# A two-layer diffusion block on one core: output weights a block ahead into four result banks, one operand sum by feature tiles, and slots of their own for the mixer's sums

## The chip, the cores and the metric

The kernel runs on 1 core of one Trainium2 chip. The metric is device time in microseconds (us) of one execution; the median of three runs is quoted. Engines are called as the profile calls them: PE is TensorE (its matmuls), PEld its weight loads, DVE is VectorE, ACT is ScalarE, POOL is GpSimd and SP is SyncE, whose queue (SPq) issues all of the loads and stores that matter here.

## The reference, cut to what matters

Two layers run over 1024 latent tokens and 256 context tokens of width 1024. The mixers of a layer (attention, mLSTM, neighbourhood) stay as they are; the change lies behind them.

```python
def trunk_layer(x, ctx, ...):
    ...
    x = x + gt1 * mix_out([ya, yb, yc, yd], g_group, w_out)      # output projection, 1024x1024
    h2 = rms_norm(x, g2) * (1 + sc2) + sh2
    x = x + gt2 * conv_ffn(h2, w_up, conv_w, conv_b, w_down)     # up 1024 -> 5632, conv, gate, down 2816 -> 1024
    if need_ctx:                                                 # layer 0 alone
        ctx = ctx + gt1c * mix_out([yac, ybc, ycc, ydc], g_group, w_out)
        h2c = rms_norm(ctx, g2) * (1 + sc2c) + sh2c
        ctx = ctx + gt2c * conv_ffn(h2c, w_up, conv_w, conv_b, w_down)
    return x, ctx

def conv_ffn(h, w_up, conv_w, conv_b, w_down):
    u = dwconv_centred(h @ w_up, conv_w, conv_b)                 # width 3, along the tokens
    gate, val = jnp.split(u, 2, axis=-1)
    return (jax.nn.silu(gate) * val) @ w_down
```

## The kernel before

Every number is kept as a high and a low part, and each product is three matmuls (`mm3`: L112 high by high, L113 the weights' high part by the data's low one, L114 the weights' low part by the data's high one). A high part is a cast on ACT, a low part a subtraction on DVE or POOL.

A layer has four stages. The first makes the projections and the mixers. **Phase 3** is the output projection with the second norm. **up** is the mixer's first product, and **down** its second.

Phase 3 (`out_span`) goes by spans of tokens: first 512 latent tokens, then 256, then the last 256 (`rest`), and in layer 0 the 256 context tokens (`cs`). For a span it loads the mixers' outputs (`yi`), transposes them on PE (`yt`), splits them (`yh`, `yl`), and then makes eight result tiles `o`, one for each feature tile f. A result tile needs two blocks of weights: a load `raw` (L100), a cast `wohi` on ACT (L103), a subtraction `wolo` on POOL or DVE (L104), in three buffers. DVE adds each result to the residual `xT` (L1476), SP stores that (L1478).

Behind a span come the norm's sums: squares `nsq` on ACT (L239), their sums over features on PE (`ssq` L243, `ss` L249), then `nms` on DVE, `nrs` on POOL (L253), `ndg` on DVE (L264), and `rsbc` on PE (L265), which spreads the factor. `scaled` then multiplies on DVE (L1489) and adds on ACT (L1490).

The up product is a Strassen form: per block j of 128 hidden features (22 of them) seven products b, of operands 11, 21, T1, T2, 22, T3, T4. T1, T2, T3 and T4 are differences of token and feature quarters. `combine` makes the parts of them that the last 512 tokens give, in two halves of 256 tokens; half 1 (`late`) belongs to `rest`. In layer 0 the context's result tiles run between the steps of half 1, in layer 1 nothing does. `kept` copies a product's bank to a tile `u` on ACT (L1588), which the later sums and the convolution read (L1602); `u` has six buffers in up's own pool.

down loads the gated values back (`graw`, L1665) with the weights (L1672) and the residual of all tokens (`xT<-sX`, eight loads at L1690), multiplies, and adds each result tile to `xT` (L1702). It works in groups of 2, 4, 4, 4, 4, 2 and 2 blocks. Up's last block and down's first tiles stand mixed in every queue. The eight result banks `b` are shared by both.

The order on each engine is static: a scheduler orders the program by priorities and its own estimates before it runs. Buffers are pools on a stack with a left and a right side; a tile that is laid over memory of a pool that is closed waits for the last users of those bytes. `xT` of down lies on the right side, where the operands 11 and 21 and up's late slots lay.

Of the kernel before, what the change touches and what calls it, by code (L numbers as in the profile page):

```python
# [7 lines left out]
F32 = mybir.dt.float32  # L8
# [7 lines left out]
P = 128  # L16
D = 1024
KD = 8
# [30 lines left out]
class Net:  # L49
# [1318 lines left out]
    def open_phase3(self, l):  # L1368
        self.spans = ([(0, 256, 1, 1024)] if self.need_ctx else []) + [(256, 768, 0, 0), (768, 1280, 0, 512)]
        self.p3 = [ExitStack() for _ in range(4)]  # L1370
        self.ring, self.late, self.made, self.B = {}, [], 0, {}
        self.operand(self.p3[2], "right", 11, 21)
        self.open_x()
        self.nrm = self.sb(self.p3[0], f"n2{l}", side="right")
        self.p3s = self.sb(self.p3[1], f"p3{l}", side="right")
        self.p3l = self.sb(self.p3[3], f"p3l{l}", side="right")
        self.p3p = self.ps(self.p3[1], f"p3m{l}", side="right")

    def operand(self, stack, side, *names):
        for b in names:  # L1380
# [3 lines left out]
    def phase3(self, l, modT):  # L1384
        spans = self.spans
        with ExitStack() as st:
            B, hc = self.B, None
# [10 lines left out]
            h = (t1 - t0) // 2  # L1398
            for _ in self.out_span(l, modT, (t0, t0 + h, v, c), (0,)):
                pass  # L1400
            rest = self.out_span(l, modT, (t0 + h, t1, v, c), (1,), (self.nc.gpsimd, self.nc.vector))
            next(rest)
            cs = self.out_span(l, modT, spans[0], None, (self.nc.gpsimd, self.nc.vector), hc) if hc else iter(())
# [11 lines left out]
            self.p3[1].close()  # L1415
            self.operand(st, None, "T4")
            few = self.need_ctx
            for x, n in (("raw", 4), ("s", 3), ("w", 3)) if few else (("raw", 4), ("s", 3), ("w", 6)):
                self.slots(st, x, n)
            with ExitStack() as mst:  # L1420
                self.slots(mst, "b", 6, "right", True)
                for half in (early, late):
                    for _ in half:
                        pass
                if hc:
                    self.norm2(l, modT, spans[0], lambda k: (hc[0][:, k], hc[1][:, k]))
                self.p3[0].close()
                self.xst.close()
                pst.close()
                self.slots(mst, "b", 2, None, True)  # L1430
                with ExitStack() as s2:
                    for x, n in (("raw", 2), ("w", 3)) if few else (("raw", 3), ("s", 1)):
                        self.slots(s2, x, n, "right", later=True)
                    self.up(l, B, hc, self.sb(s2, f"mu{l}", side="right"))
                self.p3[2].close()
                st.close()
                self.ring = {"b": self.ring["b"]}
                self.open_x()
                self.down(l, modT)

    def out_span(self, l, modT, span, homes, engs=None, home=None):
# [10 lines left out]
        for s0, long in zip(range(t0, t1, 256), homes or (1,)):  # L1452
            yh, yl = home or ((rp if long else self.p3l).tile([P, KD, 256], F32R, tag=x, name=x, bufs=1 if long else 2) for x in ("yh", "yl"))
            for i in range(s0 // P, s0 // P + 2):
                yi = self.p3l.tile([P, D], F32, tag="yi", name="yi", bufs=2)
                nc.sync.dma_start(yi, self.sY[i])
                cs = slice(i * P - s0, (i + 1) * P - s0)
                for g in range(2):
                    t = pm.tile([P, 4, P], F32, tag="yt", name="yt", bufs=1)
                    for j in range(4):  # L1460
                        nc.tensor.transpose(t[:, j], yi[:, (4 * g + j) * P:(4 * g + j + 1) * P], self.ident)
                    self.split(yh[:, 4 * g:4 * g + 4, cs], yl[:, 4 * g:4 * g + 4, cs], t)
            Y.append((yh, yl))
        yield
        for f in range(KD):
            W = []
            for x in range(2):
                hi, lo = self.weight(rp, a["w_out"][l, x * 512:(x + 1) * 512, f * P:(f + 1) * P]
                                     .rearrange("(k p) f -> p k f", p=P), engs[x], 3, "wo", 3)
                W += [(hi[:, k * P:(k + 1) * P], lo[:, k * P:(k + 1) * P]) for k in range(4)]  # L1470
            o = pm.tile([P, 512], F32, tag="o", name="o", bufs=2)
            for s, (yh, yl) in enumerate(Y):
                for k in range(KD):
                    self.mm3(o[:, s * 256:(s + 1) * 256], [(W[k], (yh[:, k], yl[:, k]))], k == 0, k == KD - 1)
# [1 line left out]
            nc.vector.scalar_tensor_tensor(out=xs, in0=o[:, 0:n], scalar=modT[:, 16 + f, v:v + 1], in1=xs,  # L1476
                                           op0=ALU.mult, op1=ALU.add)
            nc.sync.dma_start(self.sX[:, f, t0:t1], xs)  # L1478
            yield

    def scale2(self, modT, v):
# [35 lines left out]
    def combine(self, l, modT, B, half):  # L1517
# [7 lines left out]
        def sub(eng, out, a, b):  # L1525
            eng.tensor_tensor(out, a, b, ALU.subtract)

        def parts(b, x, eng):
            self.parted(x, *(y[:, :, c] for y in B[b]), eng)

        v = self.spans[-1][2]
        xs = self.xT[:, :, 768 + 256 * half:1024 + 256 * half]
        sc2 = self.scale2(modT, v)
# [2 lines left out]
        for k in range(4):  # L1536
            self.scaled(modT, xs, bc, sc2, v, k)
        yield
        sub(V, X[0, 0], X[0, 1], X[0, 0])
        yield  # L1540
        parts("T1", X[0, 0], V)
        yield
        for k in range(4, 8):
            self.scaled(modT, xs, bc, sc2, v, k)
# [15 lines left out]
    def up(self, l, B, hc, up):  # L1560
# [23 lines left out]
            self.mm3(o, [(W[k], (b[0][:, k], b[1][:, k])) for k in range(4)], first, skip_group_check=True)  # L1584

        def kept(o):
            s = up.tile([P, 512], F32, tag="u", name="u", bufs=6)
            nc.scalar.copy(out=s, in_=o)  # L1588
            return s

# [213 lines left out]
```

## Time and profile before

| what | value |
|---|---|
| median of 3 runs | 3404.1 us (3390.17 to 3408.64) |
| the profiled execution | 3407.24 us, span 3405.5 us |
| mean granted clock of PE | 0.978 |
| PE, DVE, ACT, POOL busy | 3257.6, 2215.4, 1503.2, 965.1 us |
| phase 3 of layer 0, of layer 1 (about) | 776 to 988 us, 2500 to 2696 us |
| up of layer 0, of layer 1 (about) | 988 to 1558 us, 2696 to 3152 us |

The span is what the profiler saw of the program; the execution's own time has 1.7 us around it. Busy time is the time in which an engine had an instruction under way. The granted clock is 1.0 at the upper of PE's two levels and 0.5 at the lower, so a mean between them says that PE ran a part of the stretch at the lower. All times of rows count from the span's start.

### The profile page before, as it was taken

What the parts mean: (1) busy time and instruction counts of PE and PEld (TensorE: products, weight loads), DVE (VectorE), ACT (ScalarE), POOL (GpSimd) and SP (SyncE); (2) the same over time, 40 slices, a digit from 0 to 9 for tenths busy, and PEclk for the clock granted to TensorE, in tenths of its full rate; (3) what the DMA queues carried; (4) which work ended last, traced back from release to release, by engine and by line L of the source; (5) the groups of instructions that cost most, each with busy time, mean ns of one, the idle gap of its engine ahead of it and who ended that gap; (6) DMA issues with size and microseconds to landing.
All of it is one profiled execution on the core that took longest, in us unless ns stands there. A gap on an engine that the chain in (4) does not pass through costs nothing. (4 is left out here: it accounts for less than half of the span.)

```text
span 3405.5 us, 55249 instructions
## 1 busy us (share of the span) xinstructions
PE 3257.6 (96%) x20699; PEld 2735.0 (80%) x20699; DVE 2215.4 (65%) x4141; ACT 1503.2 (44%) x3037; POOL 965.1 (28%) x1067
## 2 busy tenths in 40 slices
PE   7999999999979999999999899999999799999998
PEld 4798877878868888888887698878878678888886
DVE  4456654775578777777445656645774788888755
ACT  4345424566645444443111444424575544444321
POOL 1534424231552222210000624424313623332000
PEclk8999999999989999999999999999999899999999
DMA  7624445233532221216212534246144322223521
GB/s 288 198 74 138 147 131 159 69 106 120 161 101 70 75 67 61 78 52 238 91 62 99 152 100 135 72 130 155 55 135 128 111 78 90 75 86 117 186 82 59
DMA packets 412243, 385.87 MB, mean 113 GB/s; under 512 B 118088, under 2 KB 355784, under 8 KB 405832
## 3 DMA queue, kind: packets, MB, share of 16 engines
q1 hardware_dynamic: 411976, 382.34, 35.7%
q8 instruction: 163, 2.67, 0.3%
q14 instruction: 104, 0.85, 0.1%
HBM read 287.88 MB, written 94.37 MB: 112 GB/s over the span
## 5 line engine op out<-in xcount | busy, mean ns | idle before, releaser
L1702 DVE SCALAR_TENSOR_TENSOR xT<-b,modT,xT 128x512 f32<-128x512 f32 (+1 forms) x280 | 191.5, 695 | 202.8 <-PE b L114 202.2
L113 PE MATMUL b<-g,w 128*128 128x512 f32 (+1 forms) x880 | 321.9, 368 | 0.0
L114 PE MATMUL b<-g,w 128*128 128x512 f32 (+1 forms) x880 | 320.8, 368 | 0.0
L112 PE MATMUL b<-g,w 128*128 128x512 f32 (+1 forms) x880 | 320.1, 368 | 0.0
L112 PE MATMUL pj<-whi,hh 128*128 128x512 f32 (+2 forms) x800 | 286.1, 359 | 12.3 <-ACT v L535 6.2
L113 PE MATMUL pj<-wlo,hh 128*128 128x512 f32 (+2 forms) x800 | 281.0, 352 | 4.1 <-DVE wlo L104 4.1
L114 PE MATMUL pj<-whi,hl 128*128 128x512 f32 (+2 forms) x800 | 278.9, 350 | 0.0
L1573 POOL TENSOR_TENSOR s<-raw 128x512 f32<-128x512 f32 x88 | 117.8, 1338 | 485.1 <-DVE w L1580 397.3
L112 PEld LDWEIGHTS pj<-whi,hh 128*128 128x128 f32 x800 | 155.7, 195 | 45.4 <-ACT v L535 9.2
L113 PEld LDWEIGHTS b<-g,w 128*128 128x128 f32 x880 | 165.6, 189 | 27.5
L112 PEld LDWEIGHTS b<-g,w 128*128 128x128 f32 x880 | 165.5, 189 | 27.6
L114 PEld LDWEIGHTS b<-g,w 128*128 128x128 f32 x880 | 165.3, 188 | 27.6
L113 PEld LDWEIGHTS pj<-wlo,hh 128*128 128x128 f32 x800 | 156.1, 195 | 24.0 <-DVE wlo L104 5.0
L1602 DVE SCALAR_TENSOR_TENSOR cg<-u,vec,cg 128x512 f32<-128x512 f32 (+1 forms) x176 | 166.5, 989 | 10.0 <-ACT cg L1597 10.0
L87 ACT CAST w<-raw 128x512 fp32r<-128x512 f32 x88 | 53.6, 619 | 269.8 <-PE b L114 244.1
L1580 DVE TENSOR_TENSOR w<-raw,w 128x512 fp32r<-128x512 f32 x156 | 135.8, 885 | 54.7 <-ACT w L1579 54.7
L114 PEld LDWEIGHTS pj<-whi,hl 128*128 128x128 f32 x800 | 154.9, 194 | 20.3 <-issue 1.7
L1579 ACT CAST w<-s 128x512 fp32r<-128x512 f32 x176 | 107.0, 618 | 144.4 <-PE b L114 99.9
L104 POOL TENSOR_TENSOR wolo<-raw,wohi 128x512 fp32r<-128x512 f32 x88 | 119.2, 1357 | 151.4 <-ACT wohi L103 118.2
L114 PE MATMUL o<-yh,wolo 128*128 128x256 f32 x512 | 150.8, 296 | 8.3 <-POOL wolo L104 4.8
L112 PE MATMUL o<-yh,wohi 128*128 128x256 f32 x512 | 148.4, 291 | 8.8 <-ACT wohi L103 6.4
L113 PE MATMUL o<-yl,wohi 128*128 128x256 f32 x512 | 147.6, 289 | 0.0
(371 smaller groups left out, 9800.9 us busy)
## 6 DMA issues: line engine op xcount, KB each, us to landing
wmod<-in_w_mod_dram SPq DMA_DIRECT2D x48, 1024.0 KB
raw<-in_w_up_dram SPq DMA_DIRECT2D x176, 256.0 KB
raw<-in_w_out_dram SPq DMA_DIRECT2D x112, 256.0 KB
raw<-in_w_down_dram SPq DMA_DIRECT2D x88, 256.0 KB
raw<-in_w_in_dram SPq DMA_DIRECT2D x80, 256.0 KB
sG<-cv SPq DMA_DIRECT2D x22, 640.0 KB
graw<-sG SPq DMA_DIRECT2D x22, 640.0 KB
sG<-cv SPq DMA_DIRECT2D x22, 512.0 KB
```

What stands on the lines that cost most here:

```text
L87: nc.scalar.copy(out=hi, in_=src)
L104: eng.tensor_tensor(lo[:, 0:w], raw[:, 0:w], f32v(hi[:, 0:w]), ALU.subtract)
L112: nc.tensor.matmul(out, lh, rh, start=(first and i == 0), stop=False, **kw)
L113: nc.tensor.matmul(out, lh, rl, start=False, stop=False, **kw)
L114: nc.tensor.matmul(out, ll, rh, start=False, stop=(last and i == n - 1), **kw)
L1573: nc.gpsimd.tensor_tensor(s, x, y, op)
L1579: nc.scalar.copy(out=hi, in_=src)
L1580: nc.vector.tensor_tensor(out=lo, in0=src, in1=f32v(hi), op=ALU.subtract)
L1602: nc.vector.scalar_tensor_tensor(out=o[:, x0:x1], in0=u[:, x0 - d - c:x1 - d - c], scalar=self.cw[w][:, j:j + 1], in1=o[:, x0:x1], op0=ALU ...
L1702: nc.vector.scalar_tensor_tensor(out=xs, in0=o[:, 0:t1 - t0], scalar=modT[:, 40 + f, v:v + 1], in1=xs, op0=ALU.mult, op1=ALU.add)
```

## The change

It has four edits. The weights of result tile f+1 are made ahead of the matmuls of tile f, and have four buffers where they had three (the loads keep their three). The result tiles `o` have two banks, and from `rest` on two more in a pool `p3o`, by turns; the loads `yi` come as halves of 128x512, two buffers of that size, 36 loads where there were 18. For half 1 the difference T1 is made by feature tiles of 256 tokens, subtraction, cast and subtraction apiece, instead of one subtraction of 128x1024 and one split. The six buffers of `u` become slots: two on the left with the other slots, four on the right in the stack `s2`, below the late slots of `raw`, `w` and `s`; layer 0 has two `s` slots at first and one late where it had three at first.

```diff
+        self.p3o = [self.p3p]
...
             for _ in self.out_span(l, modT, (t0, t0 + h, v, c), (0,)):
                 pass
+            self.p3o += [self.ps(self.p3[1], f"p3o{l}", side="right")]
...
-            for x, n in (("raw", 4), ("s", 3), ("w", 3)) if few else (("raw", 4), ("s", 3), ("w", 6)):
+            for x, n in (("raw", 4), ("s", 2), ("w", 3), ("u", 2)) if few else (("raw", 4), ("s", 3), ("w", 6), ("u", 2)):
                 self.slots(st, x, n)
...
                 with ExitStack() as s2:
-                    for x, n in (("raw", 2), ("w", 3)) if few else (("raw", 3), ("s", 1)):
+                    self.slots(s2, "u", 4, "right")
+                    for x, n in (("raw", 2), ("w", 3), ("s", 1)) if few else (("raw", 3), ("s", 1)):
                         self.slots(s2, x, n, "right", later=True)
...
-                yi = self.p3l.tile([P, D], F32, tag="yi", name="yi", bufs=2)
-                nc.sync.dma_start(yi, self.sY[i])
                 cs = slice(i * P - s0, (i + 1) * P - s0)
                 for g in range(2):
+                    yi = self.p3l.tile([P, 512], F32, tag="yi", name="yi", bufs=2)
+                    nc.sync.dma_start(yi, self.sY[i, :, g * 512:(g + 1) * 512])
                     t = pm.tile([P, 4, P], F32, tag="yt", name="yt", bufs=1)
                     for j in range(4):
-                        nc.tensor.transpose(t[:, j], yi[:, (4 * g + j) * P:(4 * g + j + 1) * P], self.ident)
+                        nc.tensor.transpose(t[:, j], yi[:, j * P:(j + 1) * P], self.ident)
...
-        for f in range(KD):
+
+        def weights(f):
             W = []
             for x in range(2):
                 hi, lo = self.weight(rp, a["w_out"][l, x * 512:(x + 1) * 512, f * P:(f + 1) * P]
-                                     .rearrange("(k p) f -> p k f", p=P), engs[x], 3, "wo", 3)
+                                     .rearrange("(k p) f -> p k f", p=P), engs[x], 4, "wo", 3)
                 W += [(hi[:, k * P:(k + 1) * P], lo[:, k * P:(k + 1) * P]) for k in range(4)]
-            o = pm.tile([P, 512], F32, tag="o", name="o", bufs=2)
+            return W
+
+        W = weights(0)
+        for f in range(KD):
+            then = weights(f + 1) if f < KD - 1 else None
+            o = self.p3o[f % len(self.p3o)].tile([P, 512], F32, tag="o", name="o", bufs=2)
...
+            W = then
             yield
...
+        def fine(b, x, y):
+
+            for k in range(4):
+                sub(V, x[:, k], y[:, k], x[:, k])
+                self.parted(x[:, k], *(z[:, k, c] for z in B[b]), V)
+
...
-        sub(V, X[0, 0], X[0, 1], X[0, 0])
+        if half:
+            fine("T1", X[0, 0], X[0, 1])
+        else:
+            sub(V, X[0, 0], X[0, 1], X[0, 0])
         yield
-        parts("T1", X[0, 0], V)
+        if not half:
+            parts("T1", X[0, 0], V)
...
         def kept(o):
-            s = up.tile([P, 512], F32, tag="u", name="u", bufs=6)
+            s = self.slot("u", [P, 512])
             nc.scalar.copy(out=s, in_=o)
             return s
```

Since the scheduler orders anew, instructions move at three places that the diff doesn't show.

**PE at the end of the first span, layer 0.** The last result tile of the first 512 tokens ends, and the second span (256 tokens) begins with its transposes `yt`. Of the kernel before:

```order
L114 MATMUL o<-yh,wolo 128x256
L243 MATMUL ssq<-nsq,ones 32x256 x2
L1461 MATMUL yt<-ident,yi 128x128 x4
L243 MATMUL ssq<-nsq,ones 32x256 x2
L112 MATMUL o<-yh,wohi 128x256 x2
L249 MATMUL ss<-mean,nrow 128x1 x2
L1461 MATMUL yt<-ident,yi 128x128 x4
L113 MATMUL o<-yl,wohi 128x256
...
L265 MATMUL rsbc<-ndg,ones 128x256
```

The same place of the changed kernel:

```order
L114 MATMUL o<-yh,wolo 128x256
L243 MATMUL ssq<-nsq,ones 32x256 x4
L1464 MATMUL yt<-ident,yi 128x128 x4
L243 MATMUL ssq<-nsq,ones 32x256 x4
L1464 MATMUL yt<-ident,yi 128x128 x4
L249 MATMUL ss<-mean,nrow 128x1 x2
L243 MATMUL ssq<-nsq,ones 32x256 x4
L1464 MATMUL yt<-ident,yi 128x128 x4
L265 MATMUL rsbc<-ndg,ones 128x256
L243 MATMUL ssq<-nsq,ones 32x256 x4
L112 MATMUL o<-yh,wohi 128x256 x2
```

All sums of squares, `ss`, `rsbc` and three of the four groups of transposes now stand between the last result matmul of the one span and the first of the next; before, result matmuls stood among them. In layer 1 the rows move in the same way.

**DVE in layer 1, from the norm of the last 256 tokens to the T operands.** `scaled` is the line with `sc`, the T1 difference is `xT<-xT`, its low part `hT1l`. Of the kernel before:

```order
L264 TENSOR_SCALAR ndg<-ident,nrs 128x128 x2
L1580 TENSOR_TENSOR w<-raw,w 128x512
L1489 SCALAR_TENSOR_TENSOR xT<-xT,sc_29056,rsbc 128x256 x8
L1526 TENSOR_TENSOR xT<-xT 128x4x256
L1507 TENSOR_TENSOR hT1l<-xT,hT1h 128x4x256
L1526 TENSOR_TENSOR xT<-xT 128x4x256 x2
```

The same place of the changed kernel:

```order
L264 TENSOR_SCALAR ndg<-ident,nrs 128x128 x2
L1600 TENSOR_TENSOR w<-raw,w 128x512
L1499 SCALAR_TENSOR_TENSOR xT<-xT,sc_29139,rsbc 128x256 x8
L1536 TENSOR_TENSOR xT<-xT 128x256 x4
L1517 TENSOR_TENSOR hT1l<-xT,hT1h 128x256 x2
L1600 TENSOR_TENSOR w<-raw,w 128x512
L1517 TENSOR_TENSOR hT1l<-xT,hT1h 128x256 x2
L1536 TENSOR_TENSOR xT<-xT 128x4x256
```

The one subtraction and the one split of 128x1024 have become four of each, of 128x256, with splits of up's weights `w` among them.

**SP and DVE where up of layer 0 ends and down begins.** On SP, `xT<-sX` are the residual's eight loads, `graw` and `raw` those of down. Of the kernel before:

```order
L1651 DMA sG<-cv 128x1280
L1665 DMA graw<-sG 128x1280
L1651 DMA sG<-cv 128x1280
L1672 DMA raw<-in_w_down_dram 128x512
L1665 DMA graw<-sG 128x1280
L1672 DMA raw<-in_w_down_dram 128x512 x2
L1690 DMA xT<-sX 128x1280 x5
```

The same place of the changed kernel:

```order
L1685 DMA graw<-sG 128x1280
L1692 DMA raw<-in_w_down_dram 128x512 x2
L1685 DMA graw<-sG 128x1280
L1692 DMA raw<-in_w_down_dram 128x512
L1710 DMA xT<-sX 128x1280 x8
L1671 DMA sG<-cv 128x1280
```

The residual's loads stood behind two loads `graw` and now stand behind six, and the first of them waits for DVE. On DVE, `cv` is the last block's convolution and `xT<-b` an addition of one of down's result tiles. Of the kernel before:

```order
L1602 SCALAR_TENSOR_TENSOR cg<-u,vec,cg 128x512
L1702 SCALAR_TENSOR_TENSOR xT<-b,modT,xT 128x256 x3
L1702 SCALAR_TENSOR_TENSOR xT<-b,modT,xT 128x512 x2
L1702 SCALAR_TENSOR_TENSOR xT<-b,modT,xT 128x256
L1647 SCALAR_TENSOR_TENSOR cg<-th,cg 128x1280
L1602 SCALAR_TENSOR_TENSOR cv<-u,vec,cv 128x511
```

The same place of the changed kernel:

```order
L1622 SCALAR_TENSOR_TENSOR cv<-b,vec,cv 128x511
L1622 SCALAR_TENSOR_TENSOR cv<-u,vec,cv 128x512
L88 TENSOR_TENSOR g<-graw,g 128x1280
L88 TENSOR_TENSOR w<-raw,w 128x512
L1670 TENSOR_TENSOR cv<-cg,cv 128x1280
L88 TENSOR_TENSOR g<-graw,g 128x1280
L1722 SCALAR_TENSOR_TENSOR xT<-b,modT,xT 128x256
```

Six additions stood ahead of `cg<-th` and two more inside the convolution; now none stands ahead of the last `cv<-u`, and four other instructions follow it before the first addition. In layer 1 the same rows move in the same way, with seven additions that stood ahead.

## Rows read from the trace of the kernel before

**Rows 1.** The page's busy time, share of the span and instructions of each engine:

```profile
PE 3257.6 (96%) x20699; PEld 2735.0 (80%) x20699; DVE 2215.4 (65%) x4141; ACT 1503.2 (44%) x3037; POOL 965.1 (28%) x1067
```

**Rows 2.** Stretches of time: busy time (instructions) of each engine, clock, DMA share:

```profile
core 0: us, PE busy (x) PEld busy (x) DVE busy (x) ACT busy (x) POOL busy (x), PEclk, DMA share, GB/s
1000.00:1020.00 20.00, 14.18 (x68) 11.81 (x67) 11.48 (x21) 10.57 (x24) 4.69 (x5) 0.83 0.18 54
...
1560.00:1580.00 20.00, 20.00 (x111) 17.37 (x110) 20.00 (x29) 7.39 (x9) 0.00 (x0) 1.00 0.73 269
...
2680.00:2700.00 20.00, 13.81 (x70) 11.28 (x71) 18.65 (x14) 8.84 (x14) 13.38 (x7) 0.81 0.15 47
2700.00:2720.00 20.00, 10.86 (x41) 7.26 (x39) 13.72 (x20) 8.65 (x16) 9.11 (x7) 0.76 0.23 66
2720.00:2740.00 20.00, 15.89 (x49) 11.78 (x50) 10.82 (x11) 7.30 (x12) 7.00 (x4) 0.66 0.28 79
```

**Rows 3.** PE's waits, layer 0, 770 to 1060: us in total, times, longest:

```profile
PE o L114 <- POOL wolo L104: 7.0, 5, 3.6
PE b L112 <- ACT u L1588: 5.8, 1, 5.8
```

**Rows 4.** PE's waits, layer 1, 2500 to 2790:

```profile
PE b L112 <- ACT hT1h L1506: 6.7, 1, 6.7
PE o L112 <- ACT wohi L103: 4.3, 3, 2.9
PE b L112 <- ACT w L1579: 4.3, 3, 3.4
...
PE o L112 <- DVE xT L1476: 2.1, 1, 2.1
...
PE b L113 <- DVE hT1l L1507: 1.3, 1, 1.3
...
PE yt L1461 <- DMA yi<-sY: 0.3, 1, 0.3
```

**Rows 5.** Layer 1, the norm's factor to T1, in order of time: start, us:

```profile
2711.03 0.70 PE L265 MATMUL rsbc<-ndg,ones 128*128 128x256 f32 x2 [1.51 <-DVE ndg L264]
...
2712.57 3.21 DVE L1489 SCALAR_TENSOR_TENSOR xT<-xT,sc,rsbc 128x256 f32<-128x256 f32 x8
2715.70 1.21 DVE L1526 TENSOR_TENSOR xT<-xT 128x1024 f32<-128x1024 f32 x1
```

**Rows 6.** Layer 0, end of the first span, DVE and PE: start, us:

```profile
889.46 0.67 DVE L88 TENSOR_TENSOR yl<-yt,yh 128x512 fp32r<-128x512 f32 x1
...
891.57 0.50 PE L249 MATMUL ss<-mean,nrow 128*128 128x1 f32 x4
891.93 0.64 PE L1461 MATMUL yt<-ident,yi 128*128 128x128 f32 x4
...
892.73 0.63 PE L243 MATMUL ssq<-nsq,ones 128*32 128x256 f32 x4
...
896.33 0.70 PE L265 MATMUL rsbc<-ndg,ones 128*128 128x256 f32 x2 [1.11 <-DVE ndg L264]
```

**Rows 7.** From up to down, layer 0, then layer 1, in order of time:

```profile
1544.53 2.30 SPq L1690 DMA_DIRECT2D xT<-sX  x5
...
1555.33 2.97 DVE L1702 SCALAR_TENSOR_TENSOR xT<-b,modT,xT 128x256 f32<-128x256 f32 x6
...
1558.31 0.39 PE L112 MATMUL b<-g,w 128*128 128x512 f32 x1
...
1564.29 0.74 DVE L1602 SCALAR_TENSOR_TENSOR cv<-u,vec,cv 128x512 f32<-128x512 f32 x1
...
1569.11 1.48 DVE L88 TENSOR_TENSOR g<-graw,g 128x1280 fp32r<-128x1280 f32 x1
...
3152.51 0.39 PE L113 MATMUL b<-g,w 128*128 128x512 f32 x1
...
3157.12 0.74 DVE L1602 SCALAR_TENSOR_TENSOR cv<-u,vec,cv 128x512 f32<-128x512 f32 x1
```

## The prediction

> **What bounds the kernel now.** I read the page first: PE is busy for 3257.6 of 3405.5 us, 96% [rows 1], so 148 us of idle time and what the clock takes are all that a reordering can win. Then I looked for where PE idles. In stretches of 20 us it is full almost everywhere; it falls where phase 3 ends and up begins, in both layers: 14.18 of 20 us in layer 0 at 1000, and 13.81, 10.86 and 15.89 in layer 1 at 2680 to 2740, at a mean clock of 0.83, 0.81, 0.76 and 0.66 [rows 2]. From up to down PE doesn't idle at all, but there DVE is full too: 20.00 of 20 us at 1560 [rows 2]. The lists of waits then say what ended the idle time [rows 3, 4], and single stretches in order of time say what a wait is made of [rows 5 to 7].
>
> **The slots of u.** In layer 0 the product T2 of the first block waits 5.8 us for the copy `u` on ACT, because that waits for memory and then stands behind the context's casts [rows 3]. With its own room the copy follows up's first weight casts on ACT, ahead of those. That gives back 5.8, and about 1 of the clock: at 0.83 for 14.18 us of work [rows 2] the stretch loses 14.18 x 0.17 = 2.4 us to it, of which I take under half. The context's operands may wait instead, for 0 to 2. I take 6, between 4 and 8.
>
> **T1 by feature tiles.** In layer 1 PE waits 6.7 us for `hT1h`, 1.3 for `hT1l` and 4.3 for weights behind these on ACT and DVE [rows 4]. From the end of `rsbc` (2711.03 + 0.70) to the first hT1 product at 2718.45, the 6.7 us hold scaling on DVE (3.21), one subtraction (1.21), and two casts on ACT [rows 5]. By tiles the subtraction and cast of the first tile need a quarter of these (0.3 each), so the first hT1 product can start about 5.3 us behind `rsbc` in place of 6.7; and the changed order puts twelve h11 matmuls (12 x 0.23 = 2.8 us at full clock) between them, which before ran ahead of `rsbc`. What is left to wait is about 2.5, so 6.7 + 1.3 - 2.5 = 5.5 is won, some 2 of the 4.3 for weights, and 1.5 of the clock: in 2700 to 2740 it takes 10.86 x 0.24 + 15.89 x 0.34 = 8.0 us [rows 2]. Sum 9, between 5 (the products that follow take over the wait) and 12. In layer 0 context matmuls cover T1, and it is worth nothing there; without that cover it would cost the same 5.5.
>
> **Weights a block ahead, four result banks.** Waits for `wolo` on POOL are 7.0 us in layer 0 [rows 3]; in layer 1 those for `wohi` are 4.3 and one for a result bank is 2.1 [rows 4]. The fourth buffer puts one more block ahead of the subtractions of `combine` on DVE and POOL, where the weights queue; but the raw loads keep three buffers, and their order against the stores on SP is as before. The bank's wait goes. I take half of the rest: 4 in layer 0 (0 to 7), and 6 in layer 1 (0 to 9, with the bank, and with `nrs`, which has one tile less of POOL's ahead of it).
>
> **The halved yi loads.** 18 more issues; an issue of the residual's loads took 2.30 / 5 = 0.46 us of SP [rows 7], so 8.3 us of SP's queue in all. PE waits 0.3 us for `yi` in the whole of layer 1's phase 3 [rows 4], so I cost them at nothing; full, uncovered, they are the 8.3. The Trainium skill (DMA: Bandwidth & Descriptors, "Rules for kernel authors") speaks against such a split: it wants at least 1 MiB in a DMA, and its section "Anatomy of one DMA" gives about 2.0 us of fixed time to each on the GpSimd path. By that estimate 18 more are 36 us if nothing hides them; the trace's 0.3 us says that other work hides what there is.
>
> **A new cluster at the end of the first span.** By the changed order, nothing of the second span's results stands among the norm's sums any more: 16 `ssq`, three groups of `yt`, `ss` and `rsbc` stand between. PE's work in it is 4 x 0.63 + 3 x 0.64 + 0.50 / 2 + 0.70 / 2 = 5.0 us [rows 6]. From the last result it takes an addition, a square, its sums and a copy, about 3.2 us by the durations around, then from `ss` to `rsbc` 896.33 - 891.57 = 4.8, and the rest of `rsbc` and of `ssq`, 0.8: 8.8 us at the least [rows 6]. With the scaling of the half before (eight instructions, 3.21 [rows 5]) and `yl` splits (0.67 each [rows 6]) ahead of `ndg` on DVE it is 12.8. So PE idles for 3.8 to 7.8 where it idled for about 1.1 [rows 6]: 2.7 to 6.7 a layer, 4.5 taken, and 1 a layer for the clock, that falls elsewhere after waits of such a length [rows 2]. Both layers: 11, between 6 and 15.
>
> **A new wait from up to down.** The residual of down is laid over the bytes where up's late slots lay. These now begin with `u`, which the last block's convolution reads to its end. So the eight loads, issued from 1544.53 before, wait for the last `cv<-u` [rows 7], and all of down's additions stand behind it on DVE. What is queued behind those loads on SP are the last block's store and the loads of later groups, four more of which have moved ahead; they aren't late. What waits is PE: its result banks come free by these additions. In layer 0 the last `cv<-u` ends at 1564.29 + 0.74 = 1565.0 [rows 7], and I keep that: eight additions leave the queue ahead of it, and about as long splits `g` and `w` take their place. Behind it stand two splits of g (1.48 each [rows 7]), one of w and the gate's product, 4.8 us, so the first addition is at about 1569.8 instead of 1555.33. PE ends T4 at 1558.31 [rows 7] with six tiles of down unadded in six of eight banks. The other two are read by the convolution until about 1563.6 and 1564.3; two tiles take 2.8 us, and the next bank is free at 1570.3. PE idles for 5.3 + 3.9 = 9.2 us. In layer 1 the convolution ends sooner, with seven additions gone from it (the last `cv<-u` at 3156.1 where it was 3157.12 [rows 7]), the first addition comes at about 3162, and PE, from 3152.51 on, has one more free bank: 6.2. The clock takes about 0.8 a layer. Sum 17, between 10 and 24. That DVE is full there before [rows 2] speaks for it: it has no time in which to catch up early. The first load's landing is hidden behind DVE's 4.8 us, if it is no longer than that. No row shows one alone; at most it is 1555.33 - 1544.53 = 10.8 [rows 7], 6.0 beyond the cover. I take nothing, since DVE was at work all the time before that addition. By the Trainium skill (DMA: Bandwidth & Descriptors, "Anatomy of one DMA") 640 KB are 2.0 + 1.5 = 3.5 us, an estimate that would fit within the cover.
>
> **The sum.** Won: 6 + 9 + 4 + 6 = 25 (9 to 36). Lost: 11 + 17 = 28 (16 to 39). Net 3 slower, so 3410 by the profiled execution's 3407.24, which lies 3.1 above the median of the runs; against the median, 3407. The measurement tells about 0.5%, 17 us, from no change (the three runs alone are 18 apart).
>
> **Rivals.**
> - **The loads of the residual land late (slower).** If the first lands 10.8 us after its issue, the additions start 6.0 us later in each layer, PE waits that much longer, and the clock, lower after a longer wait, takes 2 more in each. That is 16 on top: 3423. For it speaks that eight loads of 640 KB go out together; against it that SP's queue has nothing else to move then. From 5 us a layer over the cover on, it decides.
> - **PE is covered from up to down, and the clock stays up (faster).** If the convolution, with no additions in it, ends 3 us earlier in each layer, and the splits behind it wait for nothing, 8 of the 17 are gone; if the shorter waits of layer 1 let the clock stay at its upper level, the other 6.5 of its 8.0 and 2.6 of 2680 to 2700 come back [rows 2]. 3407 - 17 = 3390, and with the upper ends of the weights' gains (6 more) 3384. Against it: the splits stand among the convolution's steps in the order.
> - **The weights are no earlier.** With three raw buffers the loads may still set the time; then 8 of the 10 are missing: 3415.
> - **The halves of yi are late.** SP's queue, not DMA, would show it: 8.3 us more, 3415.
>
> **How the numbers follow.** The forecast, no change that can be told, has 0.48; late loads 0.24; cover and clock 0.18; weights no earlier 0.06; late halves 0.04. The predicted time is 3407. Half of each end's rival lies beyond its price, so the range goes from 3385 to 3430: 3385 leaves out about 1 in 10 below, 3430 about 1 in 10 above. Without rivals, the forecast's own is 3393 to 3421. Faster by over 0.5% (under 3387) has 0.19, slower (over 3421) 0.28 with the worse of the last two rivals, and the same 0.53.
>
> **What would show it.** T2 of the first block in layer 0 without a wait for `u`; hT1's wait in layer 1 at 2 to 3 us; waits of PE for `ndg` or `yl` of 4 us and more at about 890 and 2610; waits of PE for DVE (`xT` or `cv`) of 6 to 9 us at the first tiles of down, with the residual's loads issued 20 us later than before. It is wrong if PE runs through from up to down, if result matmuls start sooner than the order makes me think, or if the waits for weights in `rest` go altogether.

## The result, and the profile after

The changed kernel takes 3422.26 us (median of six, 3418.39 to 3425.65) where the kernel before takes 3403.95 (six, 3390.17 to 3408.64). The medians are 18.3 us apart; the ratio on record, which is not that of these two medians, is 1.0061 (95% interval 1.0047 to 1.0074), so the change is slower by some 18 to 21 us and clear of no change. The forecast was 3407; the time lies within its range, at the price of the slower rival, but not by that rival's mechanism: that the two prices meet is chance.

The table cuts both traces, and those of the experiments further down, at the same places of the program on PE: phase 3 from its first result matmul to up's first product, up to the end of its last T4, down to the last matmul of its additions' stage (in layer 1 with the final transposes), "between" from there to layer 1's first result matmul. All in us.

| kernel | phase 3, layer 0 | up, 0 | down, 0 | between | phase 3, layer 1 | up, 1 | down, 1 |
|---|---|---|---|---|---|---|---|
| before | 201.13 | 569.95 | 297.46 | 678.92 | 161.87 | 455.95 | 243.87 |
| changed | 207.38 | 568.76 | 309.94 | 680.16 | 157.30 | 453.43 | 252.39 |
| u_above | 209.31 | 566.11 | 297.46 | 673.87 | 156.63 | 454.18 | 243.86 |
| four_whole_T1 | 206.64 | 567.98 | 297.46 | 676.37 | 158.89 | 452.39 | 243.86 |
| three_wo_buffers | 204.83 | 567.72 | 297.45 | 680.94 | 161.31 | 449.65 | 245.48 |
| whole_T1 | 204.76 | 567.88 | 297.46 | 677.92 | 160.80 | 452.44 | 243.86 |
| T1_without_POOL | 206.36 | 566.08 | 297.45 | 678.02 | 162.52 | 447.98 | 243.87 |
| whole_yi | 201.75 | 566.10 | 297.46 | 677.27 | 163.35 | 451.54 | 244.82 |
| u_alone_below | 201.99 | 568.14 | 308.47 | 678.27 | 160.78 | 447.05 | 253.76 |
| u_alone_above | 200.73 | 568.05 | 297.46 | 680.71 | 163.06 | 450.98 | 243.86 |
| banks_alone | 201.46 | 567.46 | 297.46 | 677.27 | 160.76 | 453.38 | 243.87 |
| u_and_DVE_T | 200.07 | 565.99 | 297.46 | 673.80 | 161.26 | 448.80 | 243.87 |
| u_banks_tiles_DVE | 202.06 | 568.77 | 297.46 | 678.96 | 162.26 | 447.72 | 243.86 |
| u_DVE_all | 198.29 | 566.87 | 297.46 | 678.12 | 156.87 | 448.81 | 243.86 |

From before to the changed kernel, down loses 12.5 + 8.5 = 21.0 us, phase 3 loses 6.2 in layer 0 and wins 4.6 in layer 1, up wins 1.2 and 2.5. What is left (1.2 between, 3.6 won ahead of phase 3) belongs to stages whose length differs by several us from one kernel to the next, with none of these edits in them.

**From up to down.** PE's waits in the changed kernel, 1060 to 1800 us; columns as in [rows 3]. Nothing else ends a wait in these 740 us:

```profile
PE b L112 <- DVE cv L1622: 7.0, 1, 7.0
PE b L112 <- DVE xT L1722: 2.0, 1, 2.0
```

The same place of the changed kernel in order of time, on SP, DVE and PE, for layer 0, and PE's for layer 1:

```profile
1568.10 3.92 SPq L1710 DMA_DIRECT2D xT<-sX  x8
...
1567.34 0.74 DVE L1622 SCALAR_TENSOR_TENSOR cv<-u,vec,cv 128x512 f32<-128x512 f32 x1
1568.00 1.48 DVE L88 TENSOR_TENSOR g<-graw,g 128x1280 fp32r<-128x1280 f32 x1
...
1570.00 1.48 DVE L1670 TENSOR_TENSOR cv<-cg,cv 128x1280 f32<-128x1280 f32 x1
...
1572.81 2.28 DVE L1722 SCALAR_TENSOR_TENSOR xT<-b,modT,xT 128x256 f32<-128x256 f32 x4
...
1566.90 0.77 PE L112 MATMUL b<-g,w 128*128 128x512 f32 x1 [6.98 <-DVE cv L1622]
1567.47 0.63 PE L113 MATMUL b<-g,w 128*128 128x512 f32 x1
...
1570.97 0.39 PE L114 MATMUL b<-g,w 128*128 128x512 f32 x1
1573.33 0.71 PE L112 MATMUL b<-g,w 128*128 128x512 f32 x1 [1.98 <-DVE xT L1722]
...
3163.67 0.50 PE L112 MATMUL b<-g,w 128*128 128x512 f32 x1 [1.10 <-DVE cv L1622]
3170.29 0.77 PE L112 MATMUL b<-g,w 128*128 128x512 f32 x1 [4.95 <-DVE xT L1722]
```

The residual's first load leaves SP 0.02 us after the last `cv<-u` ends (1567.34 + 0.74), where before it left 20 us ahead of that [rows 7]. The first addition comes at 1572.81, behind DVE's own queue and with no wait for the load, which therefore landed within 4.7 us. PE waits 7.0 us for a bank that the convolution reads, then 2.0 for one that an addition frees, and its matmuls in between take 0.63 us apiece in place of 0.39. By stretches of the changed kernel (columns as in [rows 2]):

```profile
1560.00:1580.00 20.00, 11.12 (x40) 8.91 (x41) 19.07 (x27) 8.08 (x11) 0.00 (x0) 0.74 0.89 335
...
3160.00:3180.00 20.00, 13.94 (x53) 10.71 (x52) 17.80 (x25) 4.84 (x7) 0.00 (x0) 0.83 0.85 317
```

At 1560 PE did 111 matmuls at a clock of 1.00 before [rows 2] and does 40 at 0.74 now.

**T1 of layer 1.** The changed kernel's PE, DVE and POOL in order of time:

```profile
2719.98 1.22 PE L265 MATMUL rsbc<-ndg,ones 128*128 128x256 f32 x2 [5.64 <-DVE ndg L264]
...
2726.14 0.49 PE L112 MATMUL b<-hT1h,w 128*128 128x512 f32 x1 [0.94 <-ACT hT1h L1516]
...
2734.80 0.80 PE L113 MATMUL b<-hT1l,w 128*128 128x512 f32 x1 [4.29 <-DVE hT1l L1517]
...
2721.41 3.22 DVE L1499 SCALAR_TENSOR_TENSOR xT<-xT,sc,rsbc 128x256 f32<-128x256 f32 x8
...
2726.58 0.41 DVE L1517 TENSOR_TENSOR hT1l<-xT,hT1h 128x256 fp32r<-128x256 f32 x1
2727.37 2.12 DVE L1517 TENSOR_TENSOR hT1l<-xT,hT1h 128x256 fp32r<-128x256 f32 x1 [0.39 <-ACT hT1h L1516]
2729.42 2.84 DVE L1600 TENSOR_TENSOR w<-raw,w 128x512 fp32r<-128x512 f32 x1
2732.19 2.89 DVE L1517 TENSOR_TENSOR hT1l<-xT,hT1h 128x256 fp32r<-128x256 f32 x2
2735.00 1.21 DVE L1536 TENSOR_TENSOR xT<-xT 128x1024 f32<-128x1024 f32 x1
...
2722.72 1.28 POOL L1593 TENSOR_TENSOR s<-s,raw 128x512 f32<-128x512 f32 x1
...
2726.80 2.41 POOL L1536 TENSOR_TENSOR xT<-xT 128x1024 f32<-128x1024 f32 x1 [1.43 <-DVE xT L1536]
2729.18 2.54 POOL L1517 TENSOR_TENSOR h22l<-xT,h22h 128x1024 fp32r<-128x1024 f32 x1
2731.67 2.79 POOL L1517 TENSOR_TENSOR hT3l<-xT,hT3h 128x1024 fp32r<-128x1024 f32 x1
```

The wait of 6.7 us for `hT1h` [rows 4] has become 0.9. In its place PE waits 5.6 us for the norm's factor, which now stands ahead of the h11 products, and 4.3 for a low part of T1. PE's waits in the changed kernel over the time of [rows 4], 2500 to 2790:

```profile
PE b L113 <- DVE hT1l L1517: 6.2, 3, 4.3
PE rsbc L265 <- DVE ndg L264: 5.6, 1, 5.6
```

The first low part, alone, took 0.41 us; the second, with POOL's subtraction beside it, 2.12; `w`, otherwise 0.68 here, 2.84; the subtraction of 128x1024 at 2735.00, when POOL is done, 1.21. The second low part ends 0.3 us behind the subtraction of POOL that it began under, and `w` 0.5 behind the next. So the tiles ran into POOL.

**The cluster at the end of the first span** stands where the order put it. From the last result matmul of that span to the 96th of the next it takes 26.1 us in layer 0 and 23.1 in layer 1, where it took 21.6 and 17.5. PE's waits in the changed kernel, layer 0:

```profile
875.55 0.66 PE L1464 MATMUL yt<-ident,yi 128*128 128x128 f32 x4 [0.57 <-DVE yl L88]
876.79 0.64 PE L243 MATMUL ssq<-nsq,ones 128*32 128x256 f32 x8 [0.25 <-DVE nms L251]
878.66 0.63 PE L1464 MATMUL yt<-ident,yi 128*128 128x128 f32 x4 [1.23 <-DMA yi<-sY]
883.64 0.86 PE L1464 MATMUL yt<-ident,yi 128*128 128x128 f32 x4 [2.25 <-DVE nms L251]
```

### The profile page after: what moved, and what is told of

Same layout as the page of the kernel before. It is cut to its first block, busy times and chain, and to the rows that moved or that the text cites. A ratio compares the mean times of both kernels' runs of the same rounds, so it can differ in the third digit from the quotient of the medians.

```text
span 3422.2 us, 55308 instructions
## 1 busy us (share of the span) xinstructions
PE 3257.6 (95%) x20699; PEld 2736.2 (80%) x20699; DVE 2216.9 (65%) x4153; ACT 1502.2 (44%) x3043; POOL 965.7 (28%) x1067
## 5 line engine op out<-in xcount | busy, mean ns | idle before, releaser
L112 PE MATMUL b<-g,w 128*128 128x512 f32 (+1 forms) x880 | 324.5, 371 | 15.0 <-DVE cv L1622 8.1
L114 PE MATMUL b<-g,w 128*128 128x512 f32 (+1 forms) x880 | 324.3, 370 | 0.0
L113 PE MATMUL b<-g,w 128*128 128x512 f32 (+1 forms) x880 | 324.2, 370 | 0.0
```

The lines of the kernel that those rows point to most:

```text
L112: nc.tensor.matmul(out, lh, rh, start=(first and i == 0), stop=False, **kw)
L113: nc.tensor.matmul(out, lh, rl, start=False, stop=False, **kw)
L114: nc.tensor.matmul(out, ll, rh, start=False, stop=(last and i == n - 1), **kw)
```

## The experiments

Every kernel was timed against the kernel before on the same chip, whose medians lay between 3400.94 and 3401.70 us there. The changed kernel minus one part comes first, then parts alone.

**u_above: where u lies.**

```diff
                 with ExitStack() as s2:
-                    self.slots(s2, "u", 4, "right")
                     for x, n in (("raw", 2), ("w", 3), ("s", 1)) if few else (("raw", 3), ("s", 1)):
                         self.slots(s2, x, n, "right", later=True)
+                    self.slots(s2, "u", 4, "right")
```

Expected: 

> The changed kernel with one line moved: the four right-hand slots of u are made after the late slots of raw, w and s instead of before them, so that down's residual no longer lies over them. Theory (the wait from up to down comes of where u lies): down's eight residual loads go out about 20 us sooner again, PE's waits of 7.0 + 2.0 us in layer 0 and 1.1 + 5.0 us in layer 1 go with the lower clock behind them, and the two stretches from T4's end to the end of down take 297 and 244 us as before the change: 21 us less, about 3401. Rival (the additions come late because splits of g and w stand in front on DVE, whatever the loads wait for): the stretches stay at 310 and 252 us, 3417 to 3424.

Measured: 3401.9 us, 1.0001 of before (0.9992 to 1.0010). Down takes 297.46 and 243.86 us, as before to a hundredth. The residual's first loads and the additions of u_above:

```profile
1549.63 2.24 SPq L1710 DMA_DIRECT2D xT<-sX  x5
...
1560.17 2.97 DVE L1722 SCALAR_TENSOR_TENSOR xT<-b,modT,xT 128x256 f32<-128x256 f32 x6
```

One moved line gives back 20 us, so the place of u is the cause of the whole loss from up to down. The rival on DVE's order is not tested by itself, since that order moved back together with the loads. What the traces do show is that with `u` below the loads leave SP only at the end of the last `cv<-u`, 1568.1, so that no order on DVE could have brought an addition before that; whether DVE's splits or the first load's landing sets the 4.7 us behind it isn't parted.

**three_wo_buffers: the fourth buffer.** u_above, and:

```diff
-                                     .rearrange("(k p) f -> p k f", p=P), engs[x], 4, "wo", 3)
+                                     .rearrange("(k p) f -> p k f", p=P), engs[x], 3, "wo", 3)
```

Expected: 

> As u_above, and the weights wo again in three buffers, still made a block ahead. In the static order the cluster of sums at the end of the first span is then gone. Theory (the cluster costs about 6 us in layer 0 and less in layer 1, and the fourth buffer's gain in the last 256 tokens is about as large): from the first result matmul to up's first product 201 to 204 us in layer 0 (207 with four buffers) and 158 to 162 in layer 1 (157 with four), in all 0 to 6 us faster than u_above. Rival (the fourth buffer is the gain of the change): 5 us or more slower than u_above.

Measured: 3400.12 us, 0.9998 (0.9989 to 1.0007), 1.8 us from u_above, which is not told apart. The stages tell more. Without the fourth buffer the cluster is gone, and from its last matmul of the first span PE needs 21.5 and 16.5 us again instead of 27.1 and 23.3. Part of that is work that only moved: from the first result matmul of phase 3 to the same 96th matmul of the second span, u_above takes 115.9 and 104.0, three_wo_buffers 113.9 and 101.7, so the cluster costs 2.0 and 2.3, less than the 6 of the theory in layer 0; all of phase 3 there, 204.8 us, lies just over the 201 to 204 expected. For that, the last 256 tokens of layer 1 take 35.2 us with four buffers and 41.1 with three. And then up of layer 1 takes 454.2 with four and 449.7 with three: the factor `rsbc`, ahead of twelve h11 products, makes PE wait 5.7 us. (With T1 whole, in the next runs, three and four buffers take the same there.) The static order shows one more thing: whether the weights are written a block ahead or not moves no instruction on PE; the buffer's number does.

**whole_T1 and four_whole_T1: T1 by tiles, at three and at four buffers.** In both `combine` is as before; whole_T1 also writes the weights no block ahead (not shown here):

```diff
-        if half:
-            fine("T1", X[0, 0], X[0, 1])
-        else:
-            sub(V, X[0, 0], X[0, 1], X[0, 0])
+        sub(V, X[0, 0], X[0, 1], X[0, 0])
         yield
-        if not half:
-            parts("T1", X[0, 0], V)
+        parts("T1", X[0, 0], V)
```

Expected: 

> As three_wo_buffers, with T1 of half 1 again made whole (one subtraction and one split of 128x1024), and the weights not made a block ahead, which changed no place in the static order. Theory (tiles win next to nothing in layer 1, since the four low parts run beside POOL's subtractions, where they took 5.59 us for four against 0.41 for one alone): up of layer 1 takes 449 to 453 us (449.65 by tiles), and the time is 3399 to 3404. Rival (tiles are worth the 9 us that the prediction gave them): up of layer 1 takes 457 to 460 us, the time is 3408 to 3411.

> u_above with T1 of half 1 made whole again (four weight buffers stay). Theory (with four buffers the tiles win nothing, since the norm's factor stands ahead of twelve h11 products on PE and its wait of 5.7 us stays, and POOL slows the low parts): up of layer 1 takes 453 to 457 us (454.18 by tiles). Rival (tiles are worth the 9 us of the prediction): 461 to 464.

Measured: whole_T1 3403.86 us, 1.0003 (0.9994 to 1.0012), up of layer 1 at 452.4 us against 449.7 by tiles; four_whole_T1 3404.70 us, 1.0012 (1.0002 to 1.0021), up of layer 1 at 452.4 against 454.2 by tiles. So tiles are worth 2.8 us there at three buffers, and cost 1.8 at four, as far as single profiles tell: banks_alone, further down, moves this stage by 2.4 with an edit that ends ahead of it. four_whole_T1 came out a little under the theory's 453, on the far side from the rival's.

**T1_without_POOL: who slows the tiles.** three_wo_buffers, and:

```diff
-        parts(22, X[1, 1], G)
-        sub(G, X[0, 1], X[1, 1], X[0, 1])
+        E = V if half and not self.need_ctx else G
+        parts(22, X[1, 1], E)
+        sub(E, X[0, 1], X[1, 1], X[0, 1])
...
-        parts("T3", X[0, 1], G)
+        parts("T3", X[0, 1], E)
```

Expected: 

> As three_wo_buffers, with the three instructions of POOL in half 1 of layer 1 (low part of 22, difference and low part of T3) on DVE instead, so that nothing runs on POOL beside T1's tiles. Theory (DVE's instructions with two operands in SBUF are slowed by POOL's beside them): the four low parts of T1 take 1.5 to 1.8 us together instead of 5.59, the two subtractions of 128x1024 behind them 1.2 each instead of 4.53 for two, the waits for hT1l fall under 1 us each or become one of up to 2.5 behind h22's low part, which then stands ahead on DVE, and up of layer 1 takes 446 to 449 us. Rival (the small instructions are slow in themselves, or wait for ACT): they take as long as before, DVE has three instructions more, and up of layer 1 takes 453 us and more.

Measured: 3398.63 us, 0.9992 (0.9983 to 1.0001), up of layer 1 at 448.0 us. DVE of three_wo_buffers, with POOL at work beside it:

```profile
2714.36 5.59 DVE L1517 TENSOR_TENSOR hT1l<-xT,hT1h 128x256 fp32r<-128x256 f32 x4
2719.87 4.53 DVE L1536 TENSOR_TENSOR xT<-xT 128x1024 f32<-128x1024 f32 x2
```

and of T1_without_POOL:

```profile
2711.54 1.22 DVE L1517 TENSOR_TENSOR h22l<-xT,h22h 128x1024 fp32r<-128x1024 f32 x1
2712.67 1.22 DVE L1536 TENSOR_TENSOR xT<-xT 128x1024 f32<-128x1024 f32 x1
2713.81 1.42 DVE L1517 TENSOR_TENSOR hT1l<-xT,hT1h 128x256 fp32r<-128x256 f32 x4
2715.15 1.21 DVE L1536 TENSOR_TENSOR xT<-xT 128x1024 f32<-128x1024 f32 x1
```

The same four instructions fall from 5.59 to 1.42 us. They aren't slow in themselves; POOL's subtractions beside them are what makes them long. One by one, three_wo_buffers shows how:

```profile
2714.10 2.40 POOL L1517 TENSOR_TENSOR h22l<-xT,h22h 128x1024 fp32r<-128x1024 f32 x1 [3.29 <-ACT h22h L1516]
2714.36 2.42 DVE L1517 TENSOR_TENSOR hT1l<-xT,hT1h 128x256 fp32r<-128x256 f32 x1
2716.46 2.53 POOL L1536 TENSOR_TENSOR xT<-xT 128x1024 f32<-128x1024 f32 x1
2716.71 2.57 DVE L1517 TENSOR_TENSOR hT1l<-xT,hT1h 128x256 fp32r<-128x256 f32 x1
...
2719.20 0.41 DVE L1517 TENSOR_TENSOR hT1l<-xT,hT1h 128x256 fp32r<-128x256 f32 x1
...
2720.15 3.17 POOL L1517 TENSOR_TENSOR hT3l<-xT,hT3h 128x1024 fp32r<-128x1024 f32 x1 [1.16 <-ACT hT3h L1516]
```

The first two low parts each begin under a subtraction of POOL and end 0.3 us after it has ended; the other two, with POOL idle, take 0.41. The time won in the stage, 1.7 us, is small, because the wait for hT1h stays at 5.3 us.

**whole_yi: the halved loads.** The kernel before with u_above's slots, the further banks and T1 by tiles; the loads `yi` of 128x1024. The diff against three_wo_buffers, without the lines that write the weights a block ahead, which whole_yi doesn't have either:

```diff
-                for g in range(2):
-                    yi = self.p3l.tile([P, 512], F32, tag="yi", name="yi", bufs=2)
-                    nc.sync.dma_start(yi, self.sY[i, :, g * 512:(g + 1) * 512])
+                yi = self.p3l.tile([P, D], F32, tag="yi", name="yi", bufs=2)
+                nc.sync.dma_start(yi, self.sY[i])
...
+                for g in range(2):
...
```

Expected: 

> The kernel before with u's slots above, the two further result banks and T1 by tiles, so three_wo_buffers with the loads yi whole again. Theory (the halves cost nothing that shows): within 3 us of three_wo_buffers, waits for yi of 0.3 us where the halves have up to 2. Rival (18 more issues on SP's queue cost their 8.3 us): 6 to 9 us faster than three_wo_buffers.

Measured: 3397.6 us, 0.9990 (0.9979 to 1.0002), 2.5 us from three_wo_buffers with intervals that overlap. From the first result matmul to the 96th of the second span layer 0 takes 111.1 us with whole loads, in the five kernels with whole loads up to here, and 113.9 with halves at three buffers; layer 1 shows no such difference (102.3 and 101.7). So the halves may cost up to 2.7 us in layer 0; the time of the whole doesn't show them. The 8.3 of SP's queue are not there.

**u_alone_below and u_alone_above: u alone, at both places.** The kernel before with only the edit of `u`, as in the change, and with the line moved as in u_above.

Expected: 

> The kernel before with the edit of u alone, its slots where the change puts them. Theory (u's slots under down's residual make the change slower, all by themselves): 15 to 21 us slower than before, 3419 to 3425, with PE's waits for cv and xT at the start of down as in the changed kernel. Rival (the wait needs the other edits' order too): within 5 us of before.

> The kernel before with the edit of u alone, its right-hand slots above the late slots. Theory (u's own room is worth what PE waited for it, less what the context's weights then cost): T2 of the first block in layer 0 no longer waits 5.8 us, the context's first products wait some 2 to 3 us instead, and the time is 0 to 6 us under that of before. Rival (the room is worth the whole 5.8 and the clock): 6 to 9 us faster.

Measured: u_alone_below 3409.08 us, 1.0024 (1.0015 to 1.0033); u_alone_above 3395.62 us, 0.9985 (0.9976 to 0.9994). In the traces down takes 308.47 + 253.76 us against 297.46 + 243.86 in u_alone_above, 20.9 more and so nearly all of the changed kernel's 21.0. But the time is only 8.1 us above before's, less than the 15 to 21 that I expected, because u's own room wins elsewhere: 1.8 us in up of layer 0 and 8.9 in up of layer 1. The latter I had not foreseen. In u_alone_above the two are 1.9 and 5.0, and the time is 5.3 us under before's: what I expected of u, in another place.

**banks_alone: two further banks.** u_alone_above with the pool p3o.

```diff
+        self.p3o = [self.p3p]
...
+            self.p3o += [self.ps(self.p3[1], f"p3o{l}", side="right")]
...
-            o = pm.tile([P, 512], F32, tag="o", name="o", bufs=2)
+            o = self.p3o[f % len(self.p3o)].tile([P, 512], F32, tag="o", name="o", bufs=2)
```

Expected: 

> u_alone_above with the two further result banks from the last 256 tokens on. Theory (the banks give back the one wait for a bank in layer 1, 2.1 us for an addition, and nothing in layer 0): phase 3 of layer 1 takes 160 to 162 us (163.06 without), the time is 3392 to 3396. Rival (the wait moves on to the weights behind it): phase 3 of layer 1 takes 163 us as without, the time is that of u_alone_above.

Measured: 3400.81 us, 0.9998 (0.9989 to 1.0006), 5.2 us slower than u_alone_above and over the 3392 to 3396 expected. Phase 3 of layer 1 took 160.8 us, 2.3 less, as expected. Where the rest went is not settled: up of layer 1 took 2.4 more, and the profile was also longer ahead of phase 3. u_banks_tiles_DVE, further down, points the same way: it has the banks and the tiles beyond u_and_DVE_T and is 3.4 us slower.

**u_and_DVE_T, u_banks_tiles_DVE and u_DVE_all: a faster version.** u_alone_above with POOL's three instructions on DVE in half 1 of layer 1, as in T1_without_POOL; whole_yi with the same; and u_alone_above with them on DVE in both halves of both layers (`E = V`).

Expected: 

> u_alone_above, with POOL's three instructions of half 1 of layer 1 on DVE, T1 whole. Theory (without POOL beside them the differences and low parts take 1.2 us each): the two subtractions that took 4.58 take 2.4, waits for hT2l go, up of layer 1 takes 446 to 449 us (450.98 with POOL), the time is 3391 to 3395. Rival (DVE is then the longer chain): 451 us and more.

> whole_yi with POOL's three instructions of half 1 of layer 1 on DVE: the edits that won, without the fourth weight buffer and the halves of yi. Theory: up of layer 1 takes 446 to 449 us (451.54 with POOL), the time is 3391 to 3396. Rival: as whole_yi, 3398.

> u_alone_above with POOL's instructions of combine on DVE in both halves and both layers. Theory (POOL's instructions beside DVE's cost more than they take off it): the subtractions of 128x1024 take 1.2 us everywhere unless a weight's low part runs on POOL beside them, phase 3 takes the same or up to 3 us less a layer, the time is 3386 to 3394. Rival (in phase 3 DVE is then late for the weights' low parts, of which it makes half): waits for wolo on DVE grow by 3 us and more a layer, the time is 3396 to 3402.

Measured: u_and_DVE_T 3392.49 us, 0.9974 (0.9965 to 0.9983); u_banks_tiles_DVE 3395.89 us, 0.9981 (0.9972 to 0.9991); u_DVE_all 3380.69 us, 0.9944 (0.9932 to 0.9956), faster than both kernels of the case. Up of layer 1 took 448.8, 447.7 and 448.8 us. The subtractions of 128x1024 on DVE, from the lists of groups by shape, first of the kernel before, then of u_DVE_all (busy time, mean ns):

```profile
L1526 DVE TENSOR_TENSOR xT<-xT 128x1024 f32<-128x1024 f32 x12 | 27.0, 2251 | 2.4 <-POOL h22l L1507 2.3
```

```profile
L1527 DVE TENSOR_TENSOR xT<-xT 128x1024 f32<-128x1024 f32 x16 | 21.1, 1318 | 0.3 <-ACT xT L1491 0.3
```

Sixteen such subtractions take 21.1 us where twelve took 27.0. DVE as a whole is busy for 2208.2 us with twelve instructions more, where u_alone_above, which differs in these alone, has 2210.7 (before 2215.4 [rows 1]). PE's waits for `wolo` on DVE are 4.6 us in layer 0 where u_and_DVE_T has 1.9, nearly what the rival had, but those for `wolo` on POOL fall from 6.5 to 3.1, and phase 3 still takes 198.3 and 156.9 us in place of the 200.7 and 163.1 of u_alone_above. The time is below what even the theory expected; against u_alone_above the 2.4 and 6.2 us of phase 3, the 2.2 of up in layer 1 and the 1.2 of up in layer 0 are 12.0 of the 14.9 us between the medians, and where the rest is isn't settled.

## Why the prediction was right in the places and wrong in the sum

The forecast was 25 won and 28 lost, no change that can be told; by the bound that it states itself (over 3421), the result is slower. That the time lies in the range is owed to the range's 45 us: of the 25 won, the stages show 8. By stages, the forecast against the two traces:

| stage | forecast | traces |
|---|---|---|
| from up to down, both layers | +17 | +21.0 |
| phase 3, layer 0 (cluster 5.5, weights -4) | +1.5 | +6.2 |
| phase 3, layer 1 (cluster 5.5, weights -6) | -0.5 | -4.6 |
| up, layer 0 (u) | -6 | -1.2 |
| up, layer 1 (T1) | -9 | -2.5 |

**The new wait from up to down** held, and u_above shows its cause. The waits were to be 9.2 and 6.2 us; they are 8.96 and 6.05. In layer 0 that fits so well by luck: the parts were to be 5.3 and 3.9, and are 7.0 and 2.0. The end of the last `cv<-u` came later than I had it (8.2 us after T4 instead of 6.7), since the splits moved ahead of the convolution as well. What was mis-sized is the clock: I gave it 0.8 us a layer, and it takes 12.5 - 9.0 = 3.5 and 8.53 - 6.05 = 2.5.

**T1 by tiles** is the step that failed most. Of 6.7 us of waits for `hT1h` and 1.3 for `hT1l`, 2.5 were to be left. The wait for `hT1h` did fall to 0.9, but those for `hT1l` rose to 6.2, and that for `rsbc` from 1.5 [rows 5] to 5.6. The prediction priced the first tile's subtraction and cast at 0.3 us each, from rows in which POOL was idle [rows 5], and gave the low parts behind them no price. In the changed kernel they run beside POOL's subtractions, and four take 0.41 + 2.12 + 2.89 = 5.4 us; T1_without_POOL shows that POOL is the reason for their length. The twelve h11 matmuls that were to cover the rest came at the price of the wait for `rsbc`, which they had covered: put behind it they cover T1, and one wait takes the other's place. With T1 whole, four_whole_T1 waits 5.8 us for `rsbc` and 2.6 for `hT1h`, whole_T1 6.1 for `hT1h` and not for `rsbc`, and both take 452.4. Of the two, the cover weighs more, as far as single profiles tell: with tiles, three buffers in place of four save 4.5 us of the stage, and T1_without_POOL saves 1.7 more. At three buffers the tiles are worth 2.8 us, at four nothing.

**u** came out as a whole near its price (6; u_alone_above 5.3), but by luck, since it isn't won where I had it: in up of layer 0 T2 waits no more, and the context's first products wait 2.4 + 0.8 + 0.5 us for weights instead, of which I had bounded 0 to 2. What it wins lies in up of layer 1, and by which instruction no run shows. In the changed kernel that is taken back: up of layer 1 takes 453 to 454 us in the kernels with four buffers and tiles, 447 to 451 with u alone. The fourth buffer can't be the only reason, since banks_alone, with three buffers and T1 whole, takes 453.4 as well.

**Weights a block ahead.** In layer 1 the last 256 tokens and the span before them take 4.4 + 1.6 = 6.0 us less, the 6 of the forecast. In layer 0 the last 256 take 3.5 less and the context 5.5 more, so the waits moved on by one span. The context's span takes 39.1 us in u_above and 35.4 in three_wo_buffers, where before it took 33.8: most of it is the fourth buffer's. Whether the halves have a part in it is not told: with whole loads it takes 34.3 in whole_yi and 35.4 in u_banks_tiles_DVE. The weights' place in the code has no part in it, by the static order.

**The cluster** is where the order showed it, and half as dear as I had it: from the first result matmul to the 96th of the second span it is 3.7 and 1.4 us with the halved loads in it, where I had 5.5 a layer. What was mis-sized is the idle time. From the last result matmul of the first span to that 96th PE idles for 5.15 and 2.46 us where it idled for 2.01 and 0.63, so 3.1 and 1.8 more in place of the 4.5 taken; the waits of 4 us for `ndg` or `yl` that were to show it didn't come, the longest wait there being 2.25 in layer 0 and 0.8 in layer 1.

**The rivals.** The slower one's time came true and its mechanism did not: the first load landed within 4.7 us in layer 0 and 5.1 in layer 1, and the longest wait of an addition for one of them was 0.45 us in layer 0. The faster one had no cover from up to down to point at. That the weights come no earlier is half true, in layer 0. The halves of yi cost 2.7 us in layer 0, the one stage that shows anything of them. The Trainium skill (DMA: Bandwidth & Descriptors, "Anatomy of one DMA") would have them, by its figure for the GpSimd path, at an estimated 36 us if nothing hid them; these loads go out from SP, and the runs show 2.7.

## What to carry to other kernels

A buffer that is given room of its own lies over something: ask which later tile takes those bytes, and which reader must be done first. Here the same edit of u won 5 us with its slots above the late ones, and lost 8 with them below. A number of buffers changes a static order as surely as a moved line, so compare orders, not only diffs. And a duration taken from a row holds for the neighbours that the row had: before pricing a smaller instruction by it, look at what the other engine does beside it in the new order.

## What the runs showed of the hardware that I had not expected

DVE's subtractions with two operands in SBUF seem to wait for POOL's, rather than to run at some lower speed beside them. Of 128x256, one takes 0.41 us with POOL idle; the two of three_wo_buffers that began under a subtraction of POOL took 2.42 and 2.57, and ended 0.3 us behind POOL's end. Of 128x1024, one takes 1.21 alone; the pair of 4.53 there ended at 2724.40, 1.1 us behind the subtraction of POOL that ended at 2723.32. So the 1.4 us that four low parts take on the mean is a mean of long and short ones, and the length of POOL's instruction is what sets the cost. The scaling, which has one operand in a result bank, took 3.22 us with POOL at work beside it and 3.21 with POOL idle [rows 5]. So work taken off DVE to POOL can cost DVE more than it takes off: with all of `combine` on DVE its busy time fell. The Trainium skill (GPSIMD Engine Reference, "1. Specifications") says that POOL's SBUF interfaces are shared with DVE's and names instructions with two SBUF inputs as those that contend. The traces agree, and the lengths above are theirs.

A stall on PE costs more than its length: behind waits of 9.0 us in layer 0, 3.5 more went to a clock that the rows show at 0.74 over 20 us, with matmuls of 0.63 us for some 3 us after the wait.
